# Another order of 16 expert pairs, and a later fetch of their stored rows

## The chip, the cores and the metric

The kernel runs on one core of a Trainium2 chip as one launch. The metric is the device time of an execution in microseconds (us), as the median of several runs. The profiled execution was recorded on the chip by the hardware profiler; all rows below come from it.

## The reference

The reference computes two layers of a streaming-encoder trunk on 512 tokens of width 1024. Each layer mixes the tokens in three ways (gated linear attention, mLSTM, latent attention), attends to 256 memory tokens, and ends with a mixture of experts. Only this last part is touched here:

```
weights = g_p * (e_p / sum(e_p))          # two experts a token, inside its best group
gate    = sum(one_hot(expert_id, 32) * weights[..., None], axis=1)
for e in range(32):
    h   = silu(t @ w_gate[e]) * (t @ w_up[e])        # 1024 -> 256
    out = out + (h @ w_down[e]) * gate[:, e:e+1]     # 256 -> 1024
x = layer_norm(ALPHA * x + out)
```

All of it is float32. Each expert has 3 MB of weights (2 MB gate and up, 1 MB down), so a layer reads 96 MB of them.

## The kernel before, in words

Each expert has 64 slots for its tokens. Two experts are worked at once (a pair, 128 slots); there are 16 pairs a layer, and four experts (a quad, two pairs) share one gather of tokens. In step p of the loop in `moe` (line 1432) TensorE (PE) does, in this order: the down projection of pair p-1 (L1387), gate and up of pair p (L1364), the gather of half of the next quad's tokens by one-hot matmuls (L1324), the turn of pair p's activations (L1377), and, between the gather's pieces, the scatter of pair p-1 (L1528). The last quad's two steps have no gather. VectorE (DVE) multiplies gate and up into the tile `e_sl` (L1372), which the turn reads.

A pair's result gets back to its tokens in one of two ways. Pairs 0 to 9 (`n_st` = 10) are *stored*: the result is copied out of PSUM (L257, L259) and written to the DRAM buffer `yd` by a DMA that ScalarE (ACT) issues (L1392). Their rows are fetched later by `stored_rows`: eight times, GpSimd (POOL) clears a page (L1497), an indirect DMA gathers 128 token rows from `yd` into it (L1498; rows of other pairs are skipped), and DVE adds the page, weighted, to the residual x (L1500). Pairs 10 to 15 are *scattered*: scaled at eviction (L1394, L1395), put on their tokens by 16 one-hot matmuls, and added to x by eight DVE instructions (L1532). The last pair's scatter also leaves the sums of the last layer norm, so it comes after every other sum.

Weights arrive by SyncE's (SP) queue in pages of 512 KB, 12 a pair, in the order of the pairs. The pages are a ring of 22 (`moe_raw`, L370): 5 of tag `e2` and 4 of `e1` (both named e in the profile), 3 each of `raw`, `whi` and `wlo`, and 4 in one big tile (T). A page is loaded again when the matmuls that read it are done. The eight pages of the stored rows come from this same ring, and the fetch is written down ahead of pair 12. In the last pair `tail` makes the ring skip the four pages of T, and in layer 0 `fill_ahead` takes T and two pages (`whi`, `wlo`) for the memory tokens (memT) of layer 1, each of which ACT and DVE then split in two (L351, L352).

Every engine works through its own queue in order. That order comes from a scheduler that reads the program; `run_of` chains the matmul runs of the steps, so that PE's order is that of the loop. An instruction that waits holds up all that stand behind it on its engine.

Of the kernel before, what the change touches and what calls it, by code (L numbers as in the profile page):

```python
# [21 lines left out]
P = 128  # L22
T = 512
NT = 4
D = 1024
# [4 lines left out]
NE = 32  # L30
# [166 lines left out]
class Chunks:  # L197


    def __init__(self, tiles, n, per):  # L200
        self.tiles, self.n, self.per = tiles, n, per
# [7 lines left out]
class K:  # L209
    def __init__(self, ctx, tc, a):  # L210
        self.tc, self.nc, self.a = tc, tc.nc, a
        self.n = 0
        self.n_e1, self.n_e2, self.n_raw = 8, 5, 0
        self.n_rw, self.n_hi, self.n_lo, self.n_fw = 3, 3, 3, 3
        self.fills = [dict(f) for f in FILLS]
        self.mark, self.marks = None, False
        self.n_gap, self.n_u1, self.n_u2, self.n_qk = 1, 12, 8, 2
        self.n_st = 10
        self.paged = {}
        pool = lambda name, bufs=1, **k: ctx.enter_context(tc.tile_pool(name=name, bufs=bufs, **k))  # L220
        self.cp = pool("cp")
        self.dp = pool("dp", space=DRAM)
        self.fb = pool("fb", 1, space=PSUM)
        self.pj = pool("pj", 3, space=PSUM)
        self.sm = pool("sm", 4, space=PSUM)
# [144 lines left out]
    def moe_raw(self):  # L370

        ring = [("e2", self.n_e2, self.e2)] * self.n_e2 + [("e1", self.n_e1, self.e1)] * (self.n_e1 - NT)
        ring += [("raw", self.n_rw, self.wp)] * self.n_rw + [("whi", self.n_hi, self.wp)] * self.n_hi
        ring += [("wlo", self.n_lo, self.wp)] * self.n_lo
        i = self.n_raw % (len(ring) + 4)
        if i == len(ring) and self.tail:
            self.n_raw += 4
            i = 0
        self.n_raw += 1
        if i < len(ring):  # L380
            tag, n, pool = ring[i]
            return self.t([P, 1024], tag, n, pool=pool)
        if i == len(ring):
            self.raw4 = self.t([P, 4, 1024], "T16", 4, pool=self.tp)
        return self.raw4[:, i - len(ring), :]
# [1032 lines left out]
    def moe(self, l, r, X, x, following):  # L1418

        nc, a = self.nc, self.a  # L1420
        s = r["s"]
        XX = self.t([P, 2, KC, 4 * CAP], "T16", 4, pool=self.tp)
        ohs = [r["oh0"]]
        add = self.gather_first(l, XX[:, 0], ohs[0], X)
        for t in range(NT):
            add(t)
        ws = self.t([P, NE // 2], "rws")
        last = NE // 2 - 1
        self.marks, before = True, None
        yd, si = self.yd[l], self.t([P, NT, 2], "rsi", dt=I32)  # L1430
        nc.vector.tensor_copy(si, s)
        for p in range(NE // 2):
            if p == self.n_st + 2:
                self.stored_rows(x, r["w"], yd, si)
            q, pr = p // 2, p % 2
            e = 2 * p
            if p == last:
                self.tail = True
                self.fill = iter(())
                if following and self.n_gap:  # L1440
                    self.fill_ahead(following)
            up, act, turn, down, y = self.experts(
                XX[:, q % 2, :, 128 * pr:128 * pr + 128], [a["gu"][l * NE + e + i] for i in range(2)],
                [a["dn"][l * NE + e + i] for i in range(2)], ws[:, p:p + 1], self.moe_raw,
                None if p < last else lambda: self.t([P, 1024], "e2", self.n_e2, pool=self.e2),
                yd[p * P:(p + 1) * P, :] if p < self.n_st else None)

            with self.run_of() as run:
                if before:
                    for hf in range(2):  # L1450
                        before[0](hf, run)
                for k in range(KC):
                    up(k, run)
            act()
            if p == 0:
                srow = self.token_rows(s) + self.token_rows(self.gates(r))
                self.residual(l, x)
            if p == 2:
                self.overflow_slots(r)

            full = []
            if q < NE // 4 - 1:
                if pr == 0:
                    ohs.append(self.slots_onehot(s, 256 * (q + 1), 256))
                full = [lambda run, c=4 * pr + i, o=ohs[-1], X2=XX[:, (q + 1) % 2]: self.gather(l, X2, o, 256, X, (c,), run)
                        for i in range(4)]
            ohT = self.onehot_rows(srow, p, ws) if p >= self.n_st else None
            with self.run_of() as run:
                for i in range(4):
                    if i == 3:  # L1470
                        turn(run)
                    for f in full[i:i + 1]:
                        f(run)
                    if before and before[2] is not None:
                        for t in (2 * i % NT, (2 * i + 1) % NT):
                            self.scatter(x, before[1], before[2], t, i // 2, run=run)
            before = down, y, ohT
        down, y, ohT = before
        self.mark, self.marks = None, False
        self.filler("x0")  # L1480
        gb = self.rows(l, 2)
        sums = self.t([P, NT, 2], "lsum")
        for hf in range(2):
            self.filler(f"x{1 + hf}")
            down(hf, [])
            for t in range(NT):
                self.scatter(x, y, ohT, t, hf, sums[:, t, hf:hf + 1])
        self.overflow(l, r, X, x, sums)
        return self.last_norm(x, gb, sums)

    def stored_rows(self, x, w, yd, si):

        nc = self.nc
        for i in range(2):
            for t in range(NT):
                v = self.moe_raw()
                nc.gpsimd.memset(v, 0.0)  # L1497
                nc.gpsimd.indirect_dma_start(v, None, yd, bass.IndirectOffsetOnAxis(ap=si[:, t, i:i + 1], axis=0),  # L1498
                                             bounds_check=self.n_st * P - 1, oob_is_err=False)
                nc.vector.scalar_tensor_tensor(x[t], v, w[:, t, i:i + 1], x[t], op0=OP.mult, op1=OP.add)  # L1500
# [163 lines left out]
    def layer(self, l, x_src, xT):  # L1664
# [32 lines left out]
        rt, self.sp = self.open("rt")  # L1697
        mp, self.mp = self.open("mp")
        e2, self.e2 = self.open("e2")
        self.n_raw, self.tail = 0, False  # L1700
        r = self.router_state(l)
        X = r["X"]
        self.proj_residual(l, PI_XO, oT, x, None, lambda t, st, gb: self.router_tile(x[t], t, st, r),
# [1 line left out]
        last = l == L - 1  # L1705
# [49 lines left out]
```

## Time and profile before

| | |
|---|---|
| median of 3 runs | 1597.37 us (1593.78 to 1598.43) |
| the profiled execution | 1596.71 us, its span 1594.9 us |
| PE busy | 94% of the span |
| DVE, ACT, POOL busy | 58%, 35%, 4% |
| DMA | 318.91 MB, mean 200 GB/s |
| expert loop, layer 0 (500 to 745 us) | PE 96% busy, DMA 99%, 382 GB/s |
| expert loop, layer 1 (1285 to 1535 us) | PE 96% busy, DMA 100%, 388 GB/s |

In the table of slices the two expert loops are the stretches where DMA shows 9 in slice after slice. Over the first 490 us its share is 0.36.

In layer 1 the loop is followed by one block for tokens beyond the 64 slots of an expert (L1567 and after); in layer 0 the trace shows none.

### The profile page before, as it was taken

Reading aid. Unit: us, or ns where it says so; the run is one execution under the profiler, and the core shown is the slowest. Engines: PE = TensorE matmul, PEld = TensorE weight load, DVE = VectorE, ACT = ScalarE, POOL = GpSimd, SP = SyncE. Lnnn points to the kernel's source line nnn. Section 1 sums busy time; section 2 is a strip of 40 time slices with the busy share of each in tenths; the row PEclk is TensorE's granted clock in tenths of the full one; section 3 lists DMA queues with packets and bytes.
Section 4 is the critical chain, followed back from the end, with each engine's and each line's share of the span. In section 5 each row is a group of like instructions: output and inputs, shape, how many; then the busy total and the mean of one; then the engine's idle time right before and its main releaser. Section 6 shows DMA issues by size and latency. Waiting matters only on the chain. (4 is left out here: it accounts for less than half of the span.)

```text
span 1594.9 us, 25206 instructions
## 1 busy us (share of the span) xinstructions
PE 1503.8 (94%) x9950; PEld 1094.2 (69%) x9950; DVE 919.4 (58%) x2050; ACT 557.7 (35%) x1006; POOL 67.5 (4%) x76
## 2 busy tenths in 40 slices
PE   8999999999999999999889999999999999998994
PEld 6888876898896544444478888659989855444542
DVE  6778678675568311164666868776665681111754
ACT  7444346324323212122363443462342232121212
POOL 0000000010000000300000000000000000003200
PEclk9999899999999999999899999999999999999997
DMA  6442220522437999997653332024224489999971
GB/s 222 147 126 86 75 72 21 173 66 93 137 113 261 411 358 389 387 408 282 227 175 93 116 103 89 27 79 140 80 93 163 159 305 378 398 388 399 409 297 53
DMA packets 95836, 318.91 MB, mean 200 GB/s; under 512 B 11704, under 2 KB 12216, under 8 KB 95588
## 3 DMA queue, kind: packets, MB, share of 16 engines
q1 hardware_dynamic: 90532, 301.36, 52.5%
q10 hardware_dynamic: 2880, 10.49, 1.6%
q0 software_dynamic: 2304, 5.43, 0.9%
q8 instruction: 79, 1.29, 0.3%
q14 instruction: 41, 0.34, 0.1%
HBM read 301.32 MB, written 18.87 MB: 201 GB/s over the span
## 5 line engine op out<-in xcount | busy, mean ns | idle before, releaser
L390 PE MATMUL pj<-whi,T 128*128 128x256 f32 x640 | 184.1, 288 | 5.0 <-ACT T L850 2.8
L392 PE MATMUL pj<-wlo,T 128*128 128x256 f32 x640 | 183.3, 287 | 4.5 <-DVE wlo L352 4.5
L391 PE MATMUL pj<-whi,T 128*128 128x256 f32 x640 | 182.9, 286 | 0.0
L390 PE MATMUL pj<-T,whi 128*128 128x512 f32 (+1 forms) x368 | 135.1, 368 | 5.5 <-ACT T L351 5.2
L1364 PE MATMUL pj<-e,T 128*64 128x512 f32 x480 | 128.7, 597 | 11.9 <-DMA e<-in_gu 11.9
L391 PE MATMUL pj<-T,wlo 128*128 128x512 f32 (+1 forms) x368 | 135.8, 369 | 2.3 <-DVE wlo L352 2.3
L1372 DVE TENSOR_TENSOR e_sl<-e_sl,pj 128x256 f32<-128x256 f32 x32 | 13.5, 422 | 215.3 <-ACT e_sl L1371 215.3
L392 PE MATMUL pj<-T,whi 128*128 128x512 f32 (+1 forms) x368 | 134.8, 367 | 0.0
L352 DVE TENSOR_TENSOR wlo<-raw,whi 128x1024 fp32r<-128x1024 f32 x86 | 104.7, 1221 | 51.9 <-ACT whi L351 51.3
L390 PEld LDWEIGHTS pj<-whi,T 128*128 128x128 f32 x640 | 124.4, 194 | 6.5 <-ACT T L850 3.0
L392 PEld LDWEIGHTS pj<-wlo,T 128*128 128x128 f32 x640 | 124.3, 194 | 5.9 <-DVE wlo L352 5.8
L1324 PEld LDWEIGHTS sm<-oh,T 128*128 128x128 f32 x896 | 111.3, 188 | 22.4 <-issue 19.5
L351 ACT CAST whi<-raw 128x1024 fp32r<-128x1024 f32 x86 | 89.9, 1048 | 104.1 <-PE pj L391 57.0
L391 PEld LDWEIGHTS pj<-whi,T 128*128 128x128 f32 x640 | 124.5, 195 | 0.2
L1324 PE MATMUL sm<-oh,T 128*128 128x256 f32 x896 | 122.1, 287 | 0.0
L1371 ACT ACTIVATE e_sl<-pj 128x256 f32<-128x256 f32 x32 | 12.3, 384 | 279.9 <-PE pj L1364 279.9
L1364 PEld LDWEIGHTS pj<-e,T 128*64 128x64 f32 x480 | 39.1, 136 | 94.4 <-issue 57.5
L1314 ACT ACTIVATE T<-sm,vec 128x256 f32<-128x256 f32 x116 | 65.3, 565 | 62.6 <-PE sm L1324 62.6
L390 PEld LDWEIGHTS pj<-T,whi 128*128 128x128 f32 x368 | 70.4, 192 | 17.1 <-ACT T L351 6.1
L391 PEld LDWEIGHTS pj<-T,wlo 128*128 128x128 f32 x368 | 70.6, 192 | 13.5 <-DVE wlo L352 2.9
L392 PEld LDWEIGHTS pj<-T,whi 128*128 128x128 f32 x368 | 70.4, 192 | 11.4 <-issue 1.1
L351 ACT CAST fwh<-fw 128x512 fp32r<-128x512 f32 x60 | 37.2, 620 | 82.0 <-PE fb L391 27.0
(495 smaller groups left out, 3138.8 us busy)
## 6 DMA issues: line engine op xcount, KB each, us to landing
e<-in_gu SPq DMA_DIRECT2D x120, 512.0 KB, 9.3
raw<-in_pieces SPq DMA_DIRECT2D x94, 512.0 KB, 3.6
e<-in_dn SPq DMA_DIRECT2D x56, 512.0 KB, 10.0
whi<-in_gu SPq DMA_DIRECT2D x38, 512.0 KB, 9.7
wlo<-in_gu SPq DMA_DIRECT2D x36, 512.0 KB, 10.1
T<-in_gu SPq DMA_DIRECT2D x36, 512.0 KB, 9.4
fw<-in_pieces SPq DMA_DIRECT2D x60, 256.0 KB, 3.0
raw<-in_gu SPq DMA_DIRECT2D x30, 512.0 KB, 7.3
```

Source lines behind the costliest of these rows:

```text
L351: self.nc.scalar.copy(hi, src)
L352: self.nc.vector.tensor_tensor(lo, src, hi, op=OP.subtract)
L390: mm(ps, a[0], b[0], start=first, stop=False)
L391: mm(ps, a[1], b[0], start=False, stop=False)
L392: return mm(ps, a[0], b[1], start=False, stop=last)
L1314: self.nc.scalar.activation(Xs[:, f, :], ps, AF.Identity, scale=v[:, VC_LG + f:VC_LG + f + 1], bias=v[:, VC_LB + f:VC_LB + f + 1])
L1324: run.append(nc.tensor.matmul(ps, X[i][t][:, f * P:(f + 1) * P], oh[:, t, :], start=i + t == 0, stop=i + t == NT))
L1364: run.append(nc.tensor.matmul(st["h"][CAP * i:CAP * i + CAP, :], Xs[:, k, i * CAP:(i + 1) * CAP], st["w"][i][:, (k % 2) * 512:(k % 2 + 1) ...
L1371: nc.scalar.activation(sl[0:R], st["h"][0:R, 0:DE], AF.Silu)
L1372: nc.vector.tensor_tensor(sl[0:R], sl[0:R], st["h"][0:R, DE:], op=OP.mult)
```

## The change

The quads are worked in the order 0, 5, 1, 2, 6, 3, 4, 7. With n for the place in the loop, the scattered pairs 10 and 11 stand at n = 2 and 3, the scattered 12 and 13 at n = 8 and 9, the scattered 14 and 15 at the end as before; the stored pairs fill the rest, pair 9 being the last of them at n = 13. `stored_rows` is called ahead of the last pair (n = 15) instead of ahead of pair 12, and takes its eight pages from the tags `whi` and `wlo` (three buffers each) by itself, no longer through the ring. The ring loses its rule for the last pair, whose weights now fall on `e2`, `e1` and `raw`.

```diff
--- before.py
+++ after.py
@@ -215,7 +215,7 @@
         self.fills = [dict(f) for f in FILLS]
         self.mark, self.marks = None, False
         self.n_gap, self.n_u1, self.n_u2, self.n_qk = 1, 12, 8, 2
-        self.n_st = 10
+        self.n_st, self.quads = 10, (0, 5, 1, 2, 6, 3, 4, 7)
         self.paged = {}
         pool = lambda name, bufs=1, **k: ctx.enter_context(tc.tile_pool(name=name, bufs=bufs, **k))
         self.cp = pool("cp")
@@ -373,9 +373,6 @@
         ring += [("raw", self.n_rw, self.wp)] * self.n_rw + [("whi", self.n_hi, self.wp)] * self.n_hi
         ring += [("wlo", self.n_lo, self.wp)] * self.n_lo
         i = self.n_raw % (len(ring) + 4)
-        if i == len(ring) and self.tail:
-            self.n_raw += 4
-            i = 0
         self.n_raw += 1
         if i < len(ring):
             tag, n, pool = ring[i]
@@ -1429,20 +1426,20 @@
         self.marks, before = True, None
         yd, si = self.yd[l], self.t([P, NT, 2], "rsi", dt=I32)
         nc.vector.tensor_copy(si, s)
-        for p in range(NE // 2):
-            if p == self.n_st + 2:
+        for n in range(NE // 2):
+
+            q, pr = n // 2, n % 2
+            p = 2 * self.quads[q] + pr
+            e = 2 * p
+            if n == last:
                 self.stored_rows(x, r["w"], yd, si)
-            q, pr = p // 2, p % 2
-            e = 2 * p
-            if p == last:
-                self.tail = True
                 self.fill = iter(())
                 if following and self.n_gap:
                     self.fill_ahead(following)
             up, act, turn, down, y = self.experts(
                 XX[:, q % 2, :, 128 * pr:128 * pr + 128], [a["gu"][l * NE + e + i] for i in range(2)],
                 [a["dn"][l * NE + e + i] for i in range(2)], ws[:, p:p + 1], self.moe_raw,
-                None if p < last else lambda: self.t([P, 1024], "e2", self.n_e2, pool=self.e2),
+                None if n < last else lambda: self.t([P, 1024], "e2", self.n_e2, pool=self.e2),
                 yd[p * P:(p + 1) * P, :] if p < self.n_st else None)
 
             with self.run_of() as run:
@@ -1452,16 +1449,16 @@
                 for k in range(KC):
                     up(k, run)
             act()
-            if p == 0:
+            if n == 0:
                 srow = self.token_rows(s) + self.token_rows(self.gates(r))
                 self.residual(l, x)
-            if p == 2:
+            if n == 2:
                 self.overflow_slots(r)
 
             full = []
             if q < NE // 4 - 1:
                 if pr == 0:
-                    ohs.append(self.slots_onehot(s, 256 * (q + 1), 256))
+                    ohs.append(self.slots_onehot(s, 256 * self.quads[q + 1], 256))
                 full = [lambda run, c=4 * pr + i, o=ohs[-1], X2=XX[:, (q + 1) % 2]: self.gather(l, X2, o, 256, X, (c,), run)
                         for i in range(4)]
             ohT = self.onehot_rows(srow, p, ws) if p >= self.n_st else None
@@ -1493,7 +1490,7 @@
         nc = self.nc
         for i in range(2):
             for t in range(NT):
-                v = self.moe_raw()
+                v = self.t([P, D], *(("whi", self.n_hi) if t % 2 else ("wlo", self.n_lo)), pool=self.wp)
                 nc.gpsimd.memset(v, 0.0)
                 nc.gpsimd.indirect_dma_start(v, None, yd, bass.IndirectOffsetOnAxis(ap=si[:, t, i:i + 1], axis=0),
                                              bounds_check=self.n_st * P - 1, oob_is_err=False)
@@ -1697,7 +1694,7 @@
         rt, self.sp = self.open("rt")
         mp, self.mp = self.open("mp")
         e2, self.e2 = self.open("e2")
-        self.n_raw, self.tail = 0, False
+        self.n_raw = 0
         r = self.router_state(l)
         X = r["X"]
         self.proj_residual(l, PI_XO, oT, x, None, lambda t, st, gb: self.router_tile(x[t], t, st, r),
```

What the scheduler makes of it is seen on two engines, in layer 0. On DVE, before, around the fetch; the rows L1372 are pair 10's and pair 11's `e_sl`, L1532 are scatter sums, e_529 to e_532 are the four tiles of x:

```order
L1372 TENSOR_TENSOR e_sl_6387<-e_sl_6387,pj_6349 128x256
L1395 SCALAR_TENSOR_TENSOR e_y_6455<-pj_6456,rws_5192,e_y_6454 128x512
L1395 SCALAR_TENSOR_TENSOR e_y_6455<-pj_6463,rws_5192,e_y_6454 128x512
L1372 TENSOR_TENSOR e_sl_6511<-e_sl_6511,pj_6470 128x256
L1532 TENSOR_TENSOR e_529_3055<-e_529_3055,sm_6532 128x512
...
L1500 SCALAR_TENSOR_TENSOR e_529_3055<-whi_6599,rw_5253,e_529_3055 128x1024
L1532 TENSOR_TENSOR e_531_3057<-e_531_3057,sm_6591 128x512
L1532 TENSOR_TENSOR e_532_3058<-e_532_3058,sm_6595 128x512
L1500 SCALAR_TENSOR_TENSOR e_530_3056<-whi_6605,rw_5253,e_530_3056 128x1024
```

Before, every sum of fetched rows stood behind pair 11's `e_sl`, a whole step after the gathers were issued. On DVE after the change, in the last steps of the loop; lines are three lower (L1369 is `e_sl`, L1497 the sum of fetched rows, L1392 an eviction of pair 14, L259 that of pair 9):

```order
L259 COPY e_y_6931<-pj_6938 128x512
L1497 SCALAR_TENSOR_TENSOR e_529_3055<-wlo_6999,rw_5253,e_529_3055 128x1024
L1497 SCALAR_TENSOR_TENSOR e_530_3056<-whi_7005,rw_5253,e_530_3056 128x1024
L1497 SCALAR_TENSOR_TENSOR e_532_3058<-whi_7017,rw_5253,e_532_3058 128x1024
L1369 TENSOR_TENSOR e_sl_6983<-e_sl_6983,pj_6945 128x256
L1497 SCALAR_TENSOR_TENSOR e_531_3057<-wlo_7011,rw_5253,e_531_3057 128x1024
...
L1392 SCALAR_TENSOR_TENSOR e_y_7057<-pj_7058,rws_5192,e_y_7056 128x512
L1392 SCALAR_TENSOR_TENSOR e_y_7057<-pj_7065,rws_5192,e_y_7056 128x512
L1497 SCALAR_TENSOR_TENSOR e_531_3057<-wlo_7035,rw_5253,e_531_3057 128x1024
L352 TENSOR_TENSOR T_1268_7047<-whi_7048,T_1268_7047 128x1024
L1497 SCALAR_TENSOR_TENSOR e_532_3058<-whi_7041,rw_5253,e_532_3058 128x1024
...
L1369 TENSOR_TENSOR e_sl_7113<-e_sl_7113,pj_7072 128x256
```

Three of the sums now stand ahead of pair 14's `e_sl` (e_sl_6983), and all eight ahead of pair 15's (e_sl_7113). The order of layer 1 is the same without the two rows L352. On SP, at the end of layer 0's loop, before (in_gu and in_dn are weights, in_memT the memory tokens):

```order
L1355 DMA raw_6997<-in_dn 128x1024
L1062 DMA whi_7048<-in_memT 128x1024
L1062 DMA wlo_7052<-in_memT 128x1024
L1355 DMA whi_7073<-in_gu 128x1024
L1355 DMA whi_7075<-in_gu 128x1024
L1355 DMA whi_7081<-in_gu 128x1024
L1355 DMA wlo_7083<-in_gu 128x1024
```

Here the third of the last pair's pages (whi_7081) takes the buffer of whi_7048. After the change, at the same place:

```order
L1352 DMA e_1253_6981<-in_dn 128x1024
L1352 DMA e_1276_7073<-in_gu 128x1024
L1059 DMA whi_7048<-in_memT 128x1024
L1059 DMA wlo_7052<-in_memT 128x1024
L1352 DMA e_1277_7075<-in_gu 128x1024
L1352 DMA e_1278_7081<-in_gu 128x1024
```

Seven of the last pair's eight gate and up pages now stand behind the two memT pages, and those take the buffers of the fetch's third and fourth page (whi_7017 and wlo_7011 in the DVE rows).

## Rows read from the trace of the kernel before

**Rows 1.** Windows: us from:to and length, busy us (instructions), clock, DMA share, GB/s.

```profile
600.00:620.00 20.00, 19.23 (x104) 9.60 (x104) 3.43 (x10) 5.30 (x11) 0.00 (x0) 1.00 1.00 383
720.00:740.00 20.00, 20.00 (x109) 10.72 (x107) 8.52 (x14) 4.39 (x8) 0.00 (x0) 1.00 1.03 409
```

**Rows 2.** Timeline of PE (start, length): gate and up of pairs 3 and 4.

```profile
540.87 0.59 PE L1364 MATMUL pj<-whi,T 128*64 128x512 f32 x1
...
555.52 4.03 PE L1364 MATMUL pj<-e,T 128*64 128x512 f32 x17
```

**Rows 3.** Timeline of PE: gate and up of pairs 13 and 14.

```profile
718.58 1.89 PE L1364 MATMUL pj<-raw,T 128*64 128x512 f32 x8
...
736.99 7.04 PE L1364 MATMUL pj<-e,T 128*64 128x512 f32 x32
```

**Rows 4.** Timeline of PE: gate and up of pairs 5 and 12.

```profile
570.18 1.89 PE L1364 MATMUL pj<-wlo,T 128*64 128x512 f32 x8
...
700.19 1.89 PE L1364 MATMUL pj<-T,T 128*64 128x512 f32 x8
```

**Rows 5.** Timeline of PE: last pages of pairs 6 and 9, brackets: idle before.

```profile
595.00 1.93 PE L1364 MATMUL pj<-whi,T 128*64 128x512 f32 x6 [0.39 <-DMA whi<-in_gu]
...
647.22 1.93 PE L1364 MATMUL pj<-e,T 128*64 128x512 f32 x6 [1.07 <-DMA e<-in_gu]
```

**Rows 6.** Timeline of PE: gate and up of pair 1 (both layers), pair 14 (layer 1).

```profile
511.55 2.31 PE L1364 MATMUL pj<-whi,T 128*64 128x512 f32 x9
...
1293.87 2.31 PE L1364 MATMUL pj<-whi,T 128*64 128x512 f32 x9
...
1518.21 7.04 PE L1364 MATMUL pj<-e,T 128*64 128x512 f32 x32
```

**Rows 7.** Timeline of PE: pair 9's down projection begins.

```profile
653.29 1.50 PE L1387 MATMUL pj<-e,e_hT 128*64 128x512 f32 x5
```

**Rows 8.** Timeline of POOL: the first two gathers of stored rows.

```profile
666.18 1.23 POOL L1498 DMA_INDIRECT whi<-yd,rsi  x1 [3.91 <-issue]
667.71 0.99 POOL L1498 DMA_INDIRECT whi<-yd,rsi  x1 [0.30 <-issue]
668.69 0.98 POOL L1497 MEMSET whi<- 128x1024 f32 x1
```

**Rows 9.** Line 1498's own answer: all 16 gathers, issue to landing.

```profile
DMA to landing us min/median/max: 9.0/10.1/10.8
```

**Rows 10.** Line 1500's own answer: sums of fetched rows, ns.

```profile
L1500 DVE SCALAR_TENSOR_TENSOR e<-whi,rw,e x6: 1277/1281/1394, 695.5 to 1480.2; 128x1024 f32<-128x1024 f32 x6
```

**Rows 11.** Page, part 5: busy us, mean ns, idle before and its cause.

```profile
L1372 DVE TENSOR_TENSOR e_sl<-e_sl,pj 128x256 f32<-128x256 f32 x32 | 13.5, 422 | 215.3 <-ACT e_sl L1371 215.3
```

**Rows 12.** Timeline of PE: a turn, and the down projection behind it.

```profile
580.36 0.38 PE L1377 MATMUL sm<-const,e_sl 128*128 128x128 f32 x2
...
581.63 3.66 PE L1387 MATMUL pj<-e,e_hT 128*64 128x512 f32 x15
```

**Rows 13.** Window of PE alone: busy us, granted clock, DMA share, GB/s.

```profile
757.00:762.00 5.00, 4.77 (x12) 0.66 1.01 385
```

**Rows 14.** Timeline of SP, layer 0: the last pair's whi pages.

```profile
733.37 20.38 SPq L1355 DMA_DIRECT2D whi<-in_gu  x3
```

**Rows 15.** Timeline of PE, layer 0: the last pair's third page, then its end.

```profile
757.23 1.56 PE L1364 MATMUL pj<-whi,T 128*64 128x512 f32 x2 [3.36 <-DMA whi<-in_gu]
...
765.91 3.04 PE L1528 MATMUL sm<-e_y,e_oT 128*128 128x512 f32 x12
```

**Rows 16.** Timeline of PE, layer 1: down of pair 14, then scatter.

```profile
1529.71 0.64 PE L1387 MATMUL pj<-e,e_hT 128*64 128x512 f32 x1
...
1540.16 3.06 PE L1528 MATMUL sm<-e_y,e_oT 128*128 128x512 f32 x12
```

**Rows 17.** DMA issues: KB each, median us to landing; the second from 1440 to 1480.

```profile
raw<-in_pieces SPq DMA_DIRECT2D x94, 512.0 KB, 3.6
...
raw<-in_dn SPq DMA_DIRECT2D x3, 512.0 KB, 16.0
```

## Prediction

> **What bounds the kernel now.** I read the windows first, then PE's timeline through both expert loops, then the queues of POOL, SP and DVE at their ends. In the windows DMA stands at its full share all through the loop, while PE loses time in the middle (19.23 of 20 us) and none later [rows 1]. PE's timeline gives the two prices behind that. A step whose predecessor is stored takes 540.87 to 555.52, 14.65 us [rows 2]; one whose predecessor is scattered takes 718.58 to 736.99, 18.41 us [rows 3]. The 16 extra matmuls are the difference.
>
> The supply has a price too. Pair 6's last page released PE at 595.00 and pair 9's at 647.22 [rows 5]: 36 pages of weights and three writes of results in 52.2 us, 1.34 us for each 512 KB. A stored pair (13 transfers) costs DMA 17.4 us, more than PE's 14.65; a scattered pair (12) costs 16.1 us, less than PE's 18.41. With ten stored pairs in a row, PE eats up its lead by pair 6 and then waits. From gate and up of pair 5 to those of pair 12 it takes 130.0 us [rows 4]; six plain steps and one with a scatter would take 106.3. So some 23.7 us a layer are lost there to weights that are late, and the scattered pairs at the end then run at PE's own pace while DMA runs ahead.
>
> **The alternation.** No matmul is added or removed. Between gate and up of the pair at n = 1 and those at n = 14 stand 13 steps, now four with a scatter: 9 x 14.65 + 4 x 18.41 = 205.5 us. From 511.55 and 1293.87 [rows 6] that is 717.1 in layer 0 and 1499.4 in layer 1, where before it was 736.99 [rows 3] and 1518.21 [rows 6]: 19.9 and 18.8 us earlier, if the weights come. Do they? From pair 6's last page, landed by 595.00, to the last page of gate and up at n = 13 there are 84 pages and three writes more than before, 87 transfers. At 1.34 us they end at 711.6; PE wants the page three quarters through a run of 7.0 us that starts at 702.4, so at 707.6. At the 409 GB/s of the later window [rows 1], 1.28 us each, they end at 706.5. The supply is therefore between 0 and 4.0 us late; I take 2. Gate and up at n = 14 then start at 719.0 and 1501.4, and the down projection of pair 9, the last stored one, 3.5 us earlier, at 715.5 and 1497.9. I count from there. The scatter sums of n = 2 and 3 cost nothing: DVE is busy 3.43 of 20 us in such a stretch [rows 1], and PE's 18.41 us already held them.
>
> **The fetch.** Here the gain meets a new wait. A gather needs all of `yd`, also the last pair's write. Before, pair 9's down projection began at 653.29 [rows 7] and the first gather was issued at 666.18 [rows 8]: 12.9 us for projection, eviction and write. The third gather follows after 1.53 for the first, 0.99 for the second and 0.98 for a clear [rows 8], at 16.4. It lands 10.1 us after its issue by the median of 16 (9.0 to 10.8) [rows 9], all of them beside a full stream of weights. Its sum takes 1.28 [rows 10] and ends at 27.8. Before, these sums cost nothing, since they stood behind pair 11's `e_sl` and the rows had long landed. Now three stand ahead of pair 14's `e_sl`, and behind that wait the whole of PE: its next instruction is the turn that reads `e_sl`, and n = 14 has neither gather nor scatter to fill the gap. `e_sl` takes 0.42 [rows 11], turn to down projection 1.27 [rows 12], so the down projection of pair 14 starts at 29.5, after an idle stretch of some 17 us.
>
> The landing is the one unknown that counts. From below it is bounded by 3.6 us, the median of a plain 512 KB load [rows 17]; from above by 16.0 us, that of weight pages which were queued beside the gathers [rows 17]. Layer 1's conditions are those of rows 9, since pair 15's eight pages of gate and up sit on free buffers and keep DMA full; I take 10.1. In layer 0 SP is held (below), the queue runs dry, and I take 8, between 3.6 and 10.1.
>
> The Trainium skill, "DMA: Bandwidth & Descriptors", section "Anatomy of one DMA — SWDGE (gpsimd) path", fits such a transfer as 2.0 us plus its bytes at 436 GB/s. For ten sixteenths of 512 KB that is an estimate of 2.8 us, far under the 10.1 of rows 9, which measure the transfer in a queue and not alone. By the rule the sum below would come to 1575.
>
> **Layer 1.** 1497.9 + 29.5 = 1527.4, against 1529.71 before [rows 16]: 2.3 earlier of the 18.8. After the idle stretch PE's clock has to come up. The trace shows it once: after 3.36 us without work [rows 15] the mean granted clock is 0.66 over five us [rows 13], between its levels of 2.4 and 1.2 GHz, so 1.7 us lost. That leaves 0.6. The second round of the fetch is hidden, but barely: clears 7 and 8 need the first two sums (24.3), the gathers go out at 26.3 and 27.6, land by 37.7, and the last sum ends at 39.0; gate and up of pair 15 end at 29.5 + 3.5 + 7.0 + 1.7 = 41.7. Layer 1 gains 0.6 us.
>
> **Layer 0.** Before, SP stood 20.38 us [rows 14], because the last pair's third `whi` page had to wait until memT was split out of that buffer. It went on at about 753.7, and PE had six pages and its gate and up done at 765.91 [rows 15]: 12.2 us. Now SP waits at the two memT pages for the fetch's third and fourth sum, with seven weight pages and four of the down projection queued behind it. The third sum ends at 16.4 + 8 + 1.28 = 25.7, `e_sl` and the fourth at 27.4, so at 742.9. One page of memT and one of weights more than before, at 1.3 each, make 12.2 + 2.6 = 14.8: 757.7, 8.2 us earlier than 765.91. PE's clock is in the 12.2 already, and the turn of pair 14 is hidden under it. What follows the last pair is the same work in both layers and moves as a whole.
>
> **The sum.** 8.2 + 0.6 = 8.8 us off the profiled execution's 1596.71 gives 1587.9; the median of the runs, 1597.37, lies 0.7 above it. I predict 1588. Of the 34.7 us by which the down projection of pair 9 is reached earlier in the two layers, about a quarter should arrive.
>
> **Rivals.** *Quick gathers.* If the rows land in 3.6 us, pair 14's down projection starts at 23.0, layer 1 gains 7.1 and layer 0 12.6: 1577. For it: at this place fewer pages are queued in layer 0. Against it: not one of 16 gathers was under 9.0 [rows 9]. The skill's rule belongs here.
>
> *The second round on the path (slower).* At 16 us a landing the first sum ends at 30.2, the last at 50.8, 3.2 us after gate and up of pair 15 at 47.6, and DVE comes to pair 15's `e_sl` only then: layer 1 at 1548.7 instead of 1540.16 [rows 16], 8.5 later, against 6.1 gained in layer 0 at 10.1: 1599. It decides from about 15 us on. For it: the weight pages beside the gathers took 16.0 [rows 17]. Against: the gathers themselves never exceeded 10.8.
>
> *The supply stays the bound.* At the 383 GB/s of the middle window [rows 1] a transfer takes 1.37, the page at n = 13 comes at 714.2, 6.6 late instead of 2, and both layers lose 4.6 each: 1597, no change; the alternation would then not remove the waits. For it: DMA stands at its full share now. Against: the pages before pair 6 came with a lead, and the scattered pairs give DMA 2.3 us each to rebuild it.
>
> **How the numbers follow.** Forecast 0.55, quick gathers 0.15, second round 0.10, supply 0.20. The forecast's own range is 1580 to 1594 (supply 0 to 4 late, layer 0's landing 3.6 to 10.1). The range reaches to the first two rivals, 1576 to 1600. What this kernel can tell from no change is 0.3%, 4.8 us. Faster by more: 0.51 of the forecast, all of the quick gathers, 0.04 of the supply case: 0.70. Within: 0.04 and 0.13: 0.17. Slower: 0.13.
>
> **What would show it.** Right: gate and up without DMA waits from n = 5 to n = 12; those at n = 14 near 719 and 1501; then PE idle for 15 us or more before a turn, in both layers, with DVE waiting on a gather; a half clock behind it; SP held at memT until the fetch's sums. Wrong: waits for pages in the middle of the loop, a turn at n = 14 that comes within 10 us of its gate and up, or a last `e_sl` that waits on the seventh or eighth gather.

## The result, and the profile after

The changed kernel takes 1608.61 us (median of four runs, 1604.67 to 1609.72), the kernel before 1597.9 beside it: a ratio of 1.0068 (95% interval 1.0043 to 1.0093), slower by some 11 us. The profiled execution took 1604.67 us, 8.0 more than that of before; its span is 1602.8. The forecast was 1588.

Four sections hold nearly all of it. U1 and U14 are the starts of gate and up at n = 1 and n = 14. S, in the table of the experiments, is the start of the second half of the last pair's scatter in layer 1.

| us | before | after | forecast |
|---|---|---|---|
| loop, U1 to U14, layer 0 | 225.4 | 217.7 | 207.5 |
| loop, U1 to U14, layer 1 | 224.3 | 217.3 | 207.5 |
| end of layer 0, U14 to U1 of layer 1 | 556.9 | 565.1 | 566.7 |
| end of layer 1, U14 to the span's end | 76.7 | 90.1 | 92.9 |

(The forecast's ends are those of before plus the price it put on the fetch: 18.0 - 8.2 = 9.8 and 16.8 - 0.6 = 16.2.) The ends came out as priced, a little better. The loop gave 7.7 and 7.0 us where 18 and 17 were expected. PE's timeline after, gate and up at n = 1 and n = 14 of each layer, which answers [rows 3, 6]:

```profile
512.58 1.46 PE L1361 MATMUL pj<-whi,T 128*64 128x512 f32 x6
...
730.31 0.59 PE L1361 MATMUL pj<-whi,T 128*64 128x512 f32 x1
...
1295.42 2.31 PE L1361 MATMUL pj<-whi,T 128*64 128x512 f32 x9
...
1512.73 0.59 PE L1361 MATMUL pj<-whi,T 128*64 128x512 f32 x1
```

The two prices of a step held (steps of 14.65 and 18.4 fill the loop), but the steps n = 8, 9 and 13 took 19.3, 19.6 and 20.6 us in layer 1, and 19.6, 19.8 and 20.5 in layer 0, waiting for pages. The windows of layer 0 say that DMA had not kept its full rate up to then: it ran dry just behind the scattered steps, near 580, 600 and 685 us. In the late steps, near 625 and 715, it was busy again, and PE stood. Windows of 5 us after the change (length, busy us of PE, PEld, DVE, ACT, POOL, then clock, DMA share, GB/s), and one of PE's waits in step 8:

```profile
575.00:580.00 5.00, 5.00 (x26) 1.66 (x26) 2.98 (x5) 0.59 (x1) 0.00 (x0) 1.00 1.01 401
580.00:585.00 5.00, 5.00 (x26) 1.70 (x24) 0.00 (x0) 0.00 (x0) 0.00 (x0) 1.00 0.41 150
...
600.00:605.00 5.00, 5.00 (x40) 4.28 (x40) 0.42 (x1) 2.73 (x6) 0.00 (x0) 1.00 0.58 189
...
625.00:630.00 5.00, 3.18 (x11) 0.66 (x8) 0.00 (x0) 0.00 (x0) 0.00 (x0) 1.00 1.01 360
...
685.00:690.00 5.00, 5.00 (x33) 3.09 (x30) 0.42 (x1) 1.27 (x3) 0.00 (x0) 1.00 0.45 122
...
715.00:720.00 5.00, 4.20 (x13) 0.85 (x10) 0.00 (x0) 0.00 (x0) 0.00 (x0) 1.00 1.02 400
```

```profile
630.17 2.38 PE L1361 MATMUL pj<-whi,T 128*64 128x512 f32 x8 [1.79 <-DMA whi<-in_gu]
```

What held SP is in a view that the prediction did not read, the waits of SP's own queue (us in total, times, the longest). Layer 0's loop before, then after:

```profile
SPq L1355 <- DMA yd<-e_y: 56.9, 10, 8.5
```

```profile
SPq L1352 <- DMA yd<-e_y: 70.6, 10, 10.5
```

The loader of weights waits for the write of stored rows, which ACT issues, once for each of the ten stored pairs, in both kernels. The scheduler's list of the changed kernel shows why. The loads and writes that SP and ACT issue take eight completion counters (DMAHW0 to 7) in turn, and each waits for the last user of its counter. Layer 0, the write of one stored pair on ACT, and SP's loads around its place:

```
ACT  L1389 DMA yd_77<-e_y_5891 128x1024 [waits DMAHW4_49,DVE_49,Activation_49]

SP   L1352 DMA e_1027_5937<-in_dn 128x1024 [waits DMAHW3_49,PE_49]
SP   L1352 DMA e_1028_5939<-in_dn 128x1024 [waits DMAHW5_49,PE_49]
     ...
SP   L1352 DMA raw_6022<-in_gu 128x1024 [waits DMAHW3_49,PE_49]
SP   L1352 DMA raw_6024<-in_gu 128x1024 [waits DMAHW4_49,PE_49]
```

Counter 4 is missing between SP's 3 and 5, since the write has it. So SP can issue seven loads past the write's place in the list, and the next, raw_6024, stays until the write has landed. In the trace (SP's queue, then ACT's; start, length):

```profile
572.44 11.74 SPq L1352 DMA_DIRECT2D raw<-in_gu  x3
584.27 0.86 SPq L1352 DMA_DIRECT2D whi<-in_gu  x2
...
588.10 13.54 SPq L1352 DMA_DIRECT2D T<-in_gu  x4
601.74 1.55 SPq L1352 DMA_DIRECT2D e<-in_gu  x3
```

```profile
579.70 0.33 ACTq L1389 DMA_DIRECT2D yd<-e_y  x1
...
594.35 0.33 ACTq L1389 DMA_DIRECT2D yd<-e_y  x1
```

The write goes out at 579.70, SP moves again near 584; the next goes out at 594.35, SP moves at 601.7. From 580 to 585 DMA stood at 0.41 of its share, and e1 will show that the pages were free. While the scattered steps let DMA run ahead, SP came to this place long before the write, and the lead was thrown away there.

The wait that the fetch was to bring came as told in layer 1; in layer 0 it was 10.16 us, where 15 or more was foretold. PE around pair 14's turn in layer 0 and layer 1 (in brackets: idle before, and what ended it), then in layer 1 pair 9's down projection, POOL's first gather, and DVE up to the `e_sl` of pair 14 and that of pair 15:

```profile
749.00 0.69 PE L1374 MATMUL sm<-const,e_sl 128*128 128x128 f32 x2 [10.16 <-DVE e_sl L1369]
750.15 6.40 PE L1384 MATMUL pj<-e,e_hT 128*64 128x512 f32 x16 [0.46 <-ACT e_hT L1376]
...
1536.59 0.69 PE L1374 MATMUL sm<-const,e_sl 128*128 128x128 f32 x2 [15.33 <-DVE e_sl L1369]
1537.74 5.17 PE L1384 MATMUL pj<-e,e_hT 128*64 128x512 f32 x16 [0.46 <-ACT e_hT L1376]
```

```profile
1509.25 1.08 PE L1384 MATMUL pj<-raw,e_hT 128*64 128x512 f32 x4
```

```profile
1521.14 1.05 POOL L1495 DMA_INDIRECT wlo<-yd,rsi  x1 [4.55 <-DMA e<-in_dn]
```

```profile
1530.29 1.28 DVE L1497 SCALAR_TENSOR_TENSOR e<-wlo,rw,e 128x1024 f32<-128x1024 f32 x1 [16.62 <-DMA wlo<-yd,rsi]
1532.49 1.28 DVE L1497 SCALAR_TENSOR_TENSOR e<-whi,rw,e 128x1024 f32<-128x1024 f32 x1 [0.93 <-DMA whi<-yd,rsi]
1534.91 1.28 DVE L1497 SCALAR_TENSOR_TENSOR e<-whi,rw,e 128x1024 f32<-128x1024 f32 x1 [1.14 <-DMA whi<-yd,rsi]
1536.12 0.41 DVE L1369 TENSOR_TENSOR e_sl<-e_sl,pj 128x256 f32<-128x256 f32 x1
...
1550.22 0.42 DVE L1369 TENSOR_TENSOR e_sl<-e_sl,pj 128x256 f32<-128x256 f32 x1 [2.04 <-ACT e_sl L1368]
```

The reader sees PE idle for 10.16 and 15.33 us ahead of a turn, three sums ahead of the `e_sl` that the turn reads, and slow down projections behind it (6.40 and 5.17 us against 3.66 [rows 12]).

### The profile page after: what moved, and what is told of

Read it like the earlier page. It is cut to its first block, busy times and chain, and to the rows that moved or that the text cites. A ratio compares the mean times of both kernels' runs of the same rounds, so it can differ in the third digit from the quotient of the medians.

```text
span 1602.8 us, 25190 instructions
## 1 busy us (share of the span) xinstructions
PE 1497.1 (93%) x9950; PEld 1094.2 (68%) x9950; DVE 921.4 (57%) x2050; ACT 557.6 (35%) x1006; POOL 66.8 (4%) x76
## 5 line engine op out<-in xcount | busy, mean ns | idle before, releaser
L352 DVE TENSOR_TENSOR wlo<-raw,whi 128x1024 fp32r<-128x1024 f32 x86 | 104.7, 1221 | 51.2 <-ACT whi L351 50.8
L1361 PE MATMUL pj<-e,T 128*64 128x512 f32 x448 | 121.9, 596 | 5.7 <-DMA e<-in_gu 5.5
L1369 DVE TENSOR_TENSOR e_sl<-e_sl,pj 128x256 f32<-128x256 f32 x32 | 13.5, 421 | 180.8 <-ACT e_sl L1368 180.8
L1368 ACT ACTIVATE e_sl<-pj 128x256 f32<-128x256 f32 x32 | 12.3, 385 | 257.9 <-PE pj L1361 257.9
L389 PEld LDWEIGHTS pj<-T,whi 128*128 128x128 f32 x368 | 69.8, 190 | 11.6 <-issue 1.2
L1384 PE MATMUL pj<-e,e_hT 128*64 128x512 f32 x232 | 69.4, 639 | 2.6 <-ACT e_hT L1376 2.6
```

Of the source, the lines that this page charges most:

```text
L352: self.nc.vector.tensor_tensor(lo, src, hi, op=OP.subtract)
L389: return mm(ps, a[0], b[1], start=False, stop=last)
L1361: run.append(nc.tensor.matmul(st["h"][CAP * i:CAP * i + CAP, :], Xs[:, k, i * CAP:(i + 1) * CAP], st["w"][i][:, (k % 2) * 512:(k % 2 + 1) ...
L1368: nc.scalar.activation(sl[0:R], st["h"][0:R, 0:DE], AF.Silu)
L1369: nc.vector.tensor_tensor(sl[0:R], sl[0:R], st["h"][0:R, DE:], op=OP.mult)
L1384: run.append(nc.tensor.matmul(po[CAP * i:CAP * i + CAP, :], st["hT"][:, k, CAP * i:CAP * i + CAP], st["w"][k][i][:, c], start=k == 0, stop ...
```

## The experiments

All times are medians; ratios are to the kernel before measured beside each run, with 95% intervals. The stretch ahead of the loop varies by itself (U1 of layer 0 between 508.4 and 512.6 us over these traces), so the table holds sections of the profiled executions, with S as above. The orders do not hold the same work in a section: with the changed kernel's order (after, e1, e3, e4, e8) four scatters lie in the loop, whose steps alone make 205.5 us, and with the other orders three, 10 x 14.65 + 3 x 18.41 = 201.7. The scatter that is missing there stands in the end.

| kernel | us | ratio | loop 0 / 1 | end 0 | U14 to S |
|---|---|---|---|---|---|
| before | 1597.9 | | 225.4 / 224.3 | 556.9 | 34.0 |
| after | 1608.6 | 1.0068 | 217.7 / 217.3 | 565.1 | 49.0 |
| e1 after, POOL writes | 1579.1 | 0.9878 | 205.5 / 205.4 | 565.8 | 45.4 |
| e2 before, POOL writes | 1580.9 | 0.9890 | 217.3 / 216.7 | 555.2 | 34.0 |
| e3 after, e_sl first | 1603.2 | 1.0025 | 218.3 / 217.7 | 564.0 | 48.6 |
| e4 after, no fetch | 1618.5 | 1.0115 | 216.9 / 217.9 | 557.0 | 37.9 |
| e5 other order, POOL writes | 1564.7 | 0.9801 | 208.9 / 209.2 | 556.5 | 35.0 |
| e6 the same, ACT writes | 1594.1 | 0.9980 | 224.1 / 226.8 | 555.9 | 35.1 |
| e7 after, old order | 1598.1 | 1.0012 | 220.6 / 220.6 | 559.1 | 43.6 |
| e8 e1 and e3 together | 1580.9 | 0.9891 | 205.5 / 205.5 | 570.3 | 48.2 |
| e9 e5, no memT ahead | 1563.0 | 0.9784 | 209.6 / 209.6 | 554.9 | 35.0 |
| e10 scattered quad first | 1571.9 | 0.9843 | 213.3 / 214.2 | 554.7 | 35.1 |
| e11 e5, fetch at n = 13 | 1573.1 | 0.9838 | 215.0 / 214.3 | 558.3 | 34.0 |

**e1 and e2: the write from another queue.** One edit, in the changed kernel and in the one before:

```diff
-                    nc.scalar.dma_start(dst, y[0])
+                    nc.gpsimd.dma_start(dst, y[0])
```

> The changed kernel with one edit: the stored rows' write to yd is issued by POOL instead of ACT. Theory A (shared completion counters): in the changed kernel SP stands 70.6 us a layer waiting for these writes, DMA runs dry behind the scattered pairs (0.41 and 0.45 of full share in 5 us) and gate and up at n = 14 starts at 730.3 and 1512.7. Then here SP's waits for yd are gone, the dips fill, those steps start 8 to 11 us earlier in both layers (720 to 722, 1502 to 1505), and the time falls from 1608.6 by 14 to 21 us to about 1590. Theory B (the ring of 22 pages is full and that is what stops SP): the dips stay, 1605 to 1612. Theory C (DMA's rate alone): the dips are noise, n = 14 moves by under 2 us, 1605 to 1612.

> The kernel before with the same single edit: yd is written from POOL's queue. Theory A: SP waited 56.9 us a layer for these writes here too, but eight loads were under way meanwhile and DMA stood at 0.96 to 1.01 of its share, so little is given back: 360 and 390 GB/s between 560 and 640 us become about 405, that is some 5 us a layer at most, 1588 to 1595. Theories B and C: no change, 1595 to 1600.

e1 takes 1579.08 us, 0.9878 (0.9842 to 0.9914): 29.5 less than the changed kernel, more than the 14 to 21 that I expected. SP's waits for writes by L1389 are gone, and two of the windows that were dry are full, as is the one of [rows 1]:

```profile
580.00:585.00 5.00, 5.00 (x34) 3.17 (x31) 0.42 (x1) 1.35 (x3) 0.00 (x0) 1.00 1.02 415
...
600.00:620.00 20.00, 20.00 (x114) 10.05 (x114) 4.21 (x11) 5.46 (x11) 0.53 (x1) 1.00 1.03 410
...
685.00:690.00 5.00, 5.00 (x26) 1.73 (x24) 0.69 (x1) 0.00 (x0) 0.53 (x1) 1.00 1.03 408
```

PE's timeline of e1, U1 and U14 of both layers:

```profile
509.36 1.03 PE L1361 MATMUL pj<-whi,T 128*64 128x512 f32 x4
...
714.81 0.59 PE L1361 MATMUL pj<-whi,T 128*64 128x512 f32 x1
...
1280.64 0.60 PE L1361 MATMUL pj<-whi,T 128*64 128x512 f32 x2
...
1486.08 0.59 PE L1361 MATMUL pj<-whi,T 128*64 128x512 f32 x1
```

205.45 and 205.44 us: the 9 x 14.65 + 4 x 18.41 = 205.5 of the prediction, with nothing late. Of the 30.3 us of span that the edit saves, the two loops give 12.3 and 11.9; 3.2 lie ahead of U1 of layer 0, and 3.7 behind U14 of layer 1 (the end of layer 0 is 0.7 longer). Theory A holds, B and C fall. The write itself is no quicker (issue to landing 7.1 us by its line's own answer, 6.9 before the edit); what has gone is SP's dependence on it. The Trainium skill, "DMA: Bandwidth & Descriptors", section "Rules for kernel authors", says that spreading transfers over the issuing engines gives no bandwidth, since they share the same 16 DMA engines, and saves only the time of issuing; by it e1 would gain next to nothing. On the rate the trace agrees (408 and 415 GB/s in these windows, 401 in the full one after the change); the gain comes from when SP may issue, which that rule does not speak of.

e2 shows that the kernel before paid as well, and more than I expected: its loops become 8.1 and 7.6 us shorter, not 5 at most, 1580.93 us, 0.9890 (0.9854 to 0.9926). The direction of theory A is right, its size here was too small. What is left of the waits in its loop is 15.6 and 15.0 us over the 201.7 of its steps, now beside a DMA at its full rate:

```profile
600.00:620.00 20.00, 19.04 (x98) 9.24 (x94) 3.84 (x10) 3.50 (x7) 0.53 (x1) 1.00 1.03 411
```

Of that 8.2 and 7.4 us stand in the step n = 11, around the fetch in its old place. With the writes out of the way, the old order and the new one end within 2 us of each other, and their intervals overlap: what the change gains in the loop (11.6 us a layer, from 217 to 205.4) is lost at the two ends (10.6 and 11.4). No run has the alternation alone, with the fetch where it was.

**e3 and e4: the fetch.** e3 places the sums behind pair 14's `e_sl`, e4 leaves the fetch out:

```diff
e3
-                nc.vector.scalar_tensor_tensor(x[t], v, w[:, t, i:i + 1], x[t], op0=OP.mult, op1=OP.add)
+                with self.tc.issue_after(self.sl_last.ins):
+                    nc.vector.scalar_tensor_tensor(x[t], v, w[:, t, i:i + 1], x[t], op0=OP.mult, op1=OP.add)
e4
-                self.stored_rows(x, r["w"], yd, si)
```

> The changed kernel with the eight sums of fetched rows placed behind pair 14's e_sl on DVE, nothing else. Theory A (the sums ahead of e_sl hold PE at the turn): PE's idle of 15.3 us before the turn in layer 1 and 10.2 in layer 0 go to under 2; layer 1 ends some 10 to 13 us earlier, layer 0 by 0 to 4 (there the pages of pair 15 still wait behind memT for the same sums): 1592 to 1599. Rival (the fetch is on the path anyway, through the last scatter or through pages): PE only waits further on, 1604 to 1610.

> The changed kernel without the eight gathers of stored rows, their clears and their sums in either layer: the stored pairs' share is missing from the output. It prices the whole fetch. Theory A: layer 1 loses 15 us of idle and the slow clock behind it (15 to 17 us), layer 0 the idle before the turn and SP's stand at memT (10 to 16 us): 1576 to 1584. Rival (the late supply alone made the change slower, the fetch is as cheap as before): 1602 to 1609.

e3 takes 1603.16 us, 1.0025 (1.0006 to 1.0044), 5 less than the changed kernel and between the two ranges expected; its ends show only 1.1 and 0.4 of that. Both turns come without a wait (0.93 us of idle), and PE then waits elsewhere. Layer 0, the last pair's second page; layer 1, one of its pages and the scatter of pair 14:

```profile
755.93 3.98 PE L1361 MATMUL pj<-e,T 128*64 128x512 f32 x8 [13.69 <-DMA e<-in_gu]
...
1531.27 3.58 PE L1361 MATMUL pj<-e,T 128*64 128x512 f32 x8 [2.66 <-DMA e<-in_gu]
...
1545.95 1.25 PE L1526 MATMUL sm<-e_y,e_oT 128*128 128x512 f32 x4 [1.82 <-DVE e L1530]
```

The rival expectation was right in its mechanism: the fetch is on the path through pages and the last sums too.

e4 cannot be read by its total, which lies outside both ranges. Layer 1 works on other values without the stored share, and the block for surplus tokens ran twice; the second run begins in this row and takes some 35 us:

```profile
1574.58 3.67 PE L1332 MATMUL sm<-T,oh 128*64 128x512 f32 x8 [9.13 <-POOL oh L1545]
```

Its sections tell the price: layer 0's end is 557.0 instead of 565.1, and U14 to S is 37.9 instead of 49.0. The fetch costs 8.1 and 11.1 us where the change put it; I had expected 10 to 16 and 15 to 17.

**e7: the fetch without the alternation.**

```diff
-        self.n_st, self.quads = 10, (0, 5, 1, 2, 6, 3, 4, 7)
+        self.n_st, self.quads = 10, (0, 1, 2, 3, 4, 5, 6, 7)
```

> The changed kernel with the quads back in the order 0 to 7: the later fetch into whi and wlo, without the alternation. Theory A (the fetch's wait comes from the last stored pair's write): that write is five steps old, so PE's idle before pair 14's turn is under 3 us in both layers, and the time is that of the kernel before or a little less, 1590 to 1600. Rival (it comes from the pages: whi and wlo hold weights until pair 14 has used them): the first clear can only follow pair 13's down projection, the gathers land some 13 us into n = 14, PE idles 5 to 10 us before the turn in each layer, 1603 to 1615.

1598.14 us, 1.0012 (0.9995 to 1.0030): no change. There is no idle before pair 14's turn, so what PE waited for there was the last stored pair's write, not the pages. The sums still cost something further on, in layer 1 the evictions of pair 14 that stand behind them:

```profile
1541.27 4.95 PE L1525 MATMUL sm<-e_y,e_oT 128*128 128x512 f32 x11 [7.39 <-DVE e_y L1392]
```

The loop wins 4.8 and 3.7 us, because the fetch no longer takes pages from the ring in its midst, and the ends lose 2.2 and 9.6.

**e5, e6, e11: the last stored pair earlier.** The kernel before, with the change's loop variable, another order and POOL's write (e6: without the last edit; e11: with 13 for 14):

```diff
-        self.n_st = 10
+        self.n_st, self.quads = 10, (0, 5, 1, 2, 3, 4, 6, 7)
-            if p == self.n_st + 2:
+            if n == 14:
                 self.stored_rows(x, r["w"], yd, si)
-                    nc.scalar.dma_start(dst, y[0])
+                    nc.gpsimd.dma_start(dst, y[0])
```

> The kernel before with two edits: quads in the order 0, 5, 1, 2, 3, 4, 6, 7 (the last stored pair at n = 11, the fetch through the ring as before, now written down ahead of n = 14, three steps behind it), and yd written from POOL's queue. Theory A (shared counters, and a fetch that costs only where the gathers end late): no idle of PE before a turn; gate and up at n = 14 come 205.5 us behind those at n = 1 as in the run with the changed order and POOL's write, or up to 5 us later, since eight stored steps in a row drain the lead; against that run's 1579 the 23 us of idle before the turns are gone and memT's hold of some 5 us comes back in layer 0: 1555 to 1566. Rival (DMA at its full rate bounds any order): 1575 to 1581, as with the old order and POOL's write.

> The same order and the same place of the fetch, but yd written from ACT's queue as before. Theory A: SP's waits for yd come back at 55 to 70 us a layer, DMA runs dry behind the first scattered pairs, and most of the lead is lost: 20 to 35 us slower than the run with POOL's write, 1580 to 1597. Rival (the order is what counts, POOL's write only adds a little): within 10 us of that run.

> The order 0, 5, 1, 2, 3, 4, 6, 7 with POOL's write, and the fetch written down ahead of n = 13 instead of 14, two steps behind the last stored pair. Theory: its pages are then taken from the weights of pair 12 and 13 one step earlier, SP is held about as long, n = 13 takes its 18.4 us instead of 22.4 and 23.4, and the wait moves to another step: within 5 us of 1564.7, 1560 to 1570. Rival (rows not yet written hold SP longer): 1570 to 1580.

e5 takes 1564.65 us, 0.9801 (0.9784 to 0.9818), e6 1594.10, 0.9980 (0.9958 to 1.0001): 29 us for the queue that issues ten writes a layer, with SP's waits for them back at 63.1 and 62.7 us in e6. e5's ends are within 1 us of those of before (556.5 and 35.0), and PE does not stand before a turn. But its loops still wait. The 205.5 us of the expectation belong to the changed kernel's order; the steps of this one make 201.7, and its loops are 7.1 and 7.4 us longer, in the steps n = 12 and 13, with DMA at 408 GB/s from 685 to 720 us. POOL's queue, which carries the gathers and the tail of the last write, took 22.9% of DMA's time in that stretch, 8.0 us. That the pages came late because of this traffic is argued, not shown by a run. e11, one step earlier, takes 1573.07, 0.9838 (0.9816 to 0.9861); its expectation was wrong and the rival's time right: its loops are 6.1 and 5.1 us longer still than e5's, and the wait of the changed kernel is back. PE's timeline of e11, the turn at n = 12 in both layers:

```profile
695.95 0.69 PE L1377 MATMUL sm<-const,e_sl 128*128 128x128 f32 x2 [7.54 <-DVE e_sl L1372]
...
1468.97 0.69 PE L1377 MATMUL sm<-const,e_sl 128*128 128x128 f32 x2 [6.01 <-DVE e_sl L1372]
```

**e8, e9, e10: what is left.** e8 is e1 with the edit of e3. e9 is e5 with `n_gap` = 0, so no memory tokens are loaded at the end of layer 0. e10 is e5 with the quads (5, 0, 1, 2, 3, 4, 6, 7); its first quad works on the tokens of quad 0.

> The changed kernel with both edits of the first call: yd written from POOL's queue, and the eight sums behind pair 14's e_sl. Theory A (what counts is the last stored write, not which e_sl stands in front): in layer 1 the idle of 13.3 us before pair 14's turn goes, but pair 15's e_sl still stands behind all eight sums, the last of which ends near 1519, so layer 1 ends within 3 us of the run with POOL's write alone; in layer 0 the pages of pair 15 still follow memT: 1572 to 1580 against 1579. Rival (with the pages no longer held by ACT's write, PE uses the time it wins): 1560 to 1568.

> The order 0, 5, 1, 2, 3, 4, 6, 7 with POOL's write, and no memory tokens fetched ahead at the end of layer 0 (their first group is done in layer 1 with the others). Theory: the 3.35 us of idle in layer 0's last pair and the slow clock behind it go (5 to 7 us), and the PE work of that group, some 3 us with its waits, returns elsewhere: 1558 to 1566. Rival (it filled gaps that now stand empty at the layer's border): 1566 to 1575.

> The order 5, 0, 1, 2, 3, 4, 6, 7 with POOL's write: a scattered quad at the very start, where the ring of pages is full anyway. Theory: a scattered step lets DMA win 2.3 us only while there are free pages; at the start there are few, so the ten stored steps that follow drain the lead two steps earlier, PE waits 3 to 8 us a layer for pages from n = 9 on: 1568 to 1580. Rival (the lead is not what limits here): 1562 to 1567, as with 0, 5, 1, 2, 3, 4, 6, 7.

e8 takes 1580.89, 0.9891 (0.9854 to 0.9927), just above its range and no better than e1. The 9.5 and 13.3 us for which PE stood before the turns in e1 have moved on to the next consumers, the weight pages behind memT's in layer 0 and pair 14's evictions in layer 1:

```profile
746.38 6.31 PE L1361 MATMUL pj<-e,T 128*64 128x512 f32 x16 [16.14 <-DMA e<-in_gu]
...
1523.80 3.35 PE L1526 MATMUL sm<-e_y,e_oT 128*128 128x512 f32 x7 [7.21 <-DVE e_y L1392]
```

e9 takes 1563.00, 0.9784 (0.9762 to 0.9807), as expected, but its interval and e5's overlap; it is the quickest version measured. e10 takes 1571.87, 0.9843 (0.9812 to 0.9874): its loops are 4.4 and 5.0 us longer than e5's, late from n = 10 on. That fits its expectation, that a scattered quad pays in lead only where there are pages to run ahead into.

## Why the prediction was wrong

*The step that failed* is the supply: "The supply is therefore between 0 and 4.0 us late; I take 2." It was 12.2 and 11.8 us late (217.7 and 217.3 against 205.5). I had counted 87 transfers at 1.34 us in one unbroken stream, as if SP issued whenever a page was free. It does not; the write of each stored pair holds it, and DMA runs dry. The price itself was read from rows in which SP was held already: 1.34 us is 392 GB/s, and e1 ran at 410, with nothing late, as the lower bound of 0 would have it. Putting 12.2 and 11.8 for 2 adds 20.0 us to the forecast of 1587.9; with the fetch 4.4 cheaper than priced, and 1.0 us of a later start, that is 1604.5 against 1604.67 measured (the sections add up by themselves; what shows the cause is e1).

*The rival nearest to it*, "the supply stays the bound", had the right place and the wrong cause: not a rate of 383 GB/s but an issuer that stands still. It said 6.6 us late and 1597; it also reads [rows 1] as I did, DMA at its full share as a rate that cannot be raised. The same stretch ran at 410 GB/s in e1. Of the warnings that the prediction wrote down, "waits for pages in the middle of the loop" is the one that came true.

*The price of the steps* was right: 205.45 us in e1 to a tenth. The 23.7 us of waits in the old order are real, but not all of them are a matter of stored pairs in a row: 8.1 went with the write's queue (e2), and 7.4 stand in the step n = 11 (25.8 us for 18.4), beside the fetch, whose pages and traffic the prediction did not count there.

*The fetch in layer 1* was right: pair 9's down projection at 1509.25, the first gather at 1521.14 (+11.9; 12.9 foretold), its sum 9.2 us later (10.1), the down projection of pair 14 at +28.5 (29.5). The clock cost 1.5 us (5.17 for 3.66; 1.7 foretold). The second round stayed hidden, pair 15's `e_sl` waiting 2.04 us for its own input, so the slower rival did not happen.

*The fetch in layer 0* was right in sum (8.2 us lost at that end, 9.8 foretold), but by errors that cancel, which is luck. POOL's first gather, the sum that follows, SP's second memT page, and PE's first scatter behind the last gate and up:

```profile
738.98 1.23 POOL L1495 DMA_INDIRECT wlo<-yd,rsi  x1 [4.81 <-DMA e<-in_dn]
```

```profile
744.86 1.28 DVE L1497 SCALAR_TENSOR_TENSOR e<-wlo,rw,e 128x1024 f32<-128x1024 f32 x1 [13.61 <-DMA wlo<-yd,rsi]
```

```profile
750.21 0.33 SPq L1059 DMA_DIRECT2D wlo<-in_memT  x1
```

```profile
770.23 3.06 PE L1525 MATMUL sm<-e_y,e_oT 128*128 128x512 f32 x12
```

The landing was shorter than the 8 that I took (5.9 us from gather to sum), so SP stood at memT as described but came free 23.4 us behind pair 9's down projection (at 726.83) instead of 27.4. From there the last gate and up took 20.0 us instead of 14.8, waiting for pages behind memT's, and what follows took 2.8 us less than before the change.

*The trade* was judged too kindly. With nothing late in its loop, as in e1, the changed kernel is no faster than e2 beyond their intervals; the prediction had about a quarter of 34.7 us arrive. (Those are what gate and up at n = 14 gain in the two layers; pair 9's down projection, which the prediction names there, has moved from n = 10 to n = 14.) And the second round of the fetch, by the prediction's own terms, would be on the path from about 13 us a landing, not 15; the landings in layer 1 had a median of 10.0.

Not tried: a write left on ACT's queue with a counter of its own. That the counter holds SP is read from the list, from SP's waits and from e1, e2, e5 and e6, not from such a kernel.

## What to carry to other kernels

Before counting on a queue to run ahead, ask what the issuing engine itself waits for: a prefetch is held by a shared completion counter as firmly as by a full buffer, and a full DMA share does not exclude it: the same 20 us of the old order moved 383 GB/s at a share of 1.00 [rows 1] and 411 at 1.03 with the write on POOL (e2). A transfer that waits for compute does not belong among the counters of a prefetch stream; here moving ten writes a layer to an idle engine's queue was worth 17 us to the old order and 29 to both newer ones. And a fetch that depends on the last of a series left PE's turns alone when it was written down three steps behind it, though its loop was 7 us a layer over its own steps (e5); two steps behind it cost 4 to 8 us a layer more than that (e11), and 8 to 11 against no fetch in the changed kernel (e4).

## What was not expected of the hardware

A plain write took POOL 531 ns to issue and ACT 326, with 7.1 and 6.9 us to landing: the other queue was dearer to issue from and no slower. The gathers of the changed kernel landed in 4.3 to 12.3 us, against 9.0 to 10.8 before [rows 9]. In layer 0, where SP stood at memT and DMA moved 287 GB/s from 738 to 752 us, their median was 5.9; in layer 1, at 378 GB/s from 1520 to 1537, it was 10.0.

The longer stand did not bring the slower restart. When PE went on after 10.16 us of idle in layer 0, the granted clock was 0.50 (1.2 GHz) from 749 to 755 us and 1.00 from 756 on, and the down projection took 6.40 us; after 15.33 us in layer 1 it was 0.50 from 1536 to 1540 and 1.00 from 1541 on, and the down projection took 5.17.
